# Up product of a hybrid block's FFN: six weight operands made during row 7 of the output product, two T2 sums and one evacuation brought forward on VectorE

## The chip, the cores and the metric

One core of one Trainium2 chip runs the whole program. The metric is the device time in microseconds (us), the median of several runs; lower is better. The engines are TensorE (PE in the profile), VectorE (DVE), ScalarE (ACT), GpSimd (POOL) and the DMA queue of SyncE (SP).

## The reference

One layer of a hybrid block: a token mixer (attention and a recurrent branch, merged and multiplied by `w_o`), then a convolutional feed-forward network (FFN). All arrays are fp32; there are 1024 tokens and 1024 channels, and `D_FF` is 2816.

```python
h = h + gate1[:, None, :] * mix                  # mix = merged @ w_o
u2 = modulate(rms_norm(h, ln2_g[l]), shift2, scale2)
h = h + gate2[:, None, :] * conv_ffn(u2, w_up[l], conv_w[l], conv_b[l], w_down[l])

def conv_ffn(u, w_up, conv_w, conv_b, w_down):
    a, b = jnp.split(u @ w_up, 2, axis=-1)
    a = conv(a, conv_w) + conv_b                 # depthwise, three tokens
    return (jax.nn.silu(a) * b) @ w_down
```

The change lies where the product with `w_o` (the output product) ends and the product with `w_up` (the Up product) begins.

## The kernel before

**fp32 in three passes.** An fp32 operand is split into a part `hi` (rounded to the fast matmul type, a cast on ScalarE) and a rest `lo` (operand minus `hi`, on VectorE; this document calls that instruction the operand's *lower*). Each product of two operands is made of hi·hi, lo·hi and hi·lo (`PARTS`).

**Output product.** `wo_do(t, k)` computes 128 tokens (row t, 0 to 7): 48 matmuls, 8 parts of the contraction in the outer loop (`kt`), two halves of the channels, three passes. The weights' lo parts lie in the slots `a0` to `a7`, slot `a<kt>` being read in part kt. `wo_row(t, ps)` follows: on VectorE times `g1b` (L1459) and plus h (L1460), on ScalarE the sum of squares (L1461), then a store by SP. `norm2` adds the two halves' sums of squares (L1400) and makes 1/rms on ScalarE (L322, L323); `scale_row` multiplies the row by it (L1408; for row 7 one half on VectorE, L1411, and one on ScalarE, L1412).

**Activations of the Up product.** `turn2` transposes the scaled rows on TensorE into PSUM banks (`tr`), four 128 by 128 blocks per channel block, and evacuates them with the modulation's scale and shift: on ScalarE (L1429), or on VectorE by `evac_dve` (L1436) for the places in `by_dve`. The first half of the tokens gives B11 and B21, made earlier; the second half gives B12 (`U[0]`) and B22 (`U[1]`), four channel blocks of 512 tokens each.

**Up product in seven products.** It is done in 22 slices i; in each the 2 by 2 blocks A (weights) and B (activations) are multiplied in seven products instead of eight, with sums formed beforehand:

```python
OPS = {1: ("A11", "B11"), 2: ("A12", "B21"), 3: ("S4", "B22"), 4: ("A22", "T4"), 5: ("S1", "T1"), 6: ("S2", "T2"),
       7: ("S3", "T3")}
```

S1 = A21 + A22, S2 = S1 - A11, S3 = A11 - A21, S4 = A12 - S2; T3 = B22 - B12 (`diff`), T2 = T3 + B11, T4 = B21 - T2, T1 = B22 - T2. The T operands are made once, while slices 0 and 1 run, and serve all slices; the A and S operands are made for each slice. A product (`up_product`) is 12 matmuls of 128x128 by 128x512 on a bank X, Y or W. `plan` lists the products (i, k):

```python
plan = [(i, k) for ks in ((1, 2), (7,), (6,)) for i in range(2) for k in ks]
plan += [(0, 4), (0, 5), (1, 5), (1, 4), (0, 3), (1, 3)] + [(2, k) for k in (1, 7, 6, 2, 4, 5)]
```

So products 1 and 2 of slices 0 and 1 come first, with the transposes between them, then product 7 of both (T3), product 6 of both (T2), (0, 4) with T4, (0, 5) and (1, 5) with T1, and so on.

**Operands.** `up_ahead(n)` makes the A and S operands of the first n products of the plan: `up_make` forms a sum if one is needed (S2 at L1515, S4 at L1518), casts `hi` on ScalarE (L1522) and returns the lower (L1526) as a function that the caller runs later. From the fifth operand on they are put in the slots `a0` to `a5` in turn, which until then hold lo weights of the output product. `up_evac` takes results out of PSUM (L1600 and L1605 to L1609), `up_first` and `later` schedule the convolution of a slice: `conv_last` (L1563, ScalarE), `conv_taps` (L1560, VectorE), `silu`, `gated`; the number n in `up_first` says after how many products the chain begins. The load of slice i + 2 is issued by the lower of S4 of slice i, into buffers of slice i that are free again.

**Order.** From before row 5 on, VectorE, ScalarE and SP run exactly in the order of the code (a manual schedule), as TensorE does throughout; an instruction that waits holds all that stand behind it on its engine.

Of the kernel before, what the change touches and what calls it, by code (L numbers as in the profile page):

```python
# [12 lines left out]
ALU = mybir.AluOpType  # L13
# [121 lines left out]
def hybrid_block(ctx: ExitStack, tc: tile.TileContext, a, out):  # L135
# [13 lines left out]
    def f32(ap):  # L149
        return ap.bitcast(F32)  # L150

    tt, stt, ts = nc.vector.tensor_tensor, nc.vector.scalar_tensor_tensor, nc.vector.tensor_scalar
# [167 lines left out]
    def rms_rstd(dst, ssq):  # L320

        nc.scalar.activation(dst, ssq, AF.Ln, scale=1.0 / D, bias=epsr[:, 0:1])  # L322
        nc.scalar.activation(dst, dst, AF.Exp, scale=-0.5)  # L323
# [50 lines left out]
    with ExitStack() as es:  # L374
# [66 lines left out]
        with tc.tile_pool(name="st", bufs=1) as st, tc.tile_pool(name="stp", bufs=2, space=PS) as stp, \  # L441
                tc.manual_schedule(engines={mybir.EngineType.SP, mybir.EngineType.DVE, mybir.EngineType.Activation}):
            ssq = st.tile([128, 8], F32, name="ssq")
# [597 lines left out]
    with tc.manual_schedule(engines={mybir.EngineType.DVE, mybir.EngineType.Activation}):  # L1041
# [7 lines left out]
        def slot(free):  # L1049
            while not free:  # L1050
                yield 100
            yield free.popleft() - weave.now
# [219 lines left out]
    if "rest" in marks:  # L1272
        g, m = (gsp.tile([128, NH], F32, tag="sp0", name=f"rest{k}") for k in range(2))
        i = nc.scalar.activation(g, marks["rest"], AF.Abs)
# [13 lines left out]
    ssq = hp.tile([128, 32], F32, name="ssq2")  # L1288

    def pairs(tags, name, dt=F32R):  # L1290

        ts_ = [slot(tag, f"{name}_{tag}", dt) for tag in tags]
        return [ts_[k // 2][:, k % 2 * NH : k % 2 * NH + NH] for k in range(2 * len(tags))]

    def halves(tags, name):

        n = len(tags) // 2
        return [pairs(tags[x * n : x * n + n], f"{name}{x}") for x in range(2)]
# [98 lines left out]
    def norm2(t0, t1):  # L1397

        hs, rs = slice(t0, t1), slice(8 + t0, 8 + t1)
        tt(ssq[:, rs], ssq[:, rs], ssq[:, hs], op=ALU.add)  # L1400
        rms_rstd(ssq[:, rs], ssq[:, rs])
# [3 lines left out]
    def scale_row(t, dst=None):  # L1405
        r = ssq[:, 8 + t : 9 + t]
        if dst is None:
            ts(h_sb[t], h_sb[t], r, None, op0=ALU.mult)  # L1408
            dst = [h_sb[t][:, c * NH : c * NH + NH] for c in range(2)]
        else:  # L1410
            ts(dst[0], h_sb[t][:, 0:NH], r, None, op0=ALU.mult)  # L1411
            nc.scalar.activation(dst[1], h_sb[t][:, NH:], AF.Copy, scale=r)  # L1412
        normed[t] = dst
# [20 lines left out]
    def evac_dve(n):  # L1434
        dst, ps, A, B = put[n]
        ts(dst, ps, A, B, op0=ALU.mult, op1=ALU.add)  # L1436
# [17 lines left out]
    def wo_row(t, ps):  # L1454

        for c in range(2):
            cs = slice(c * NH, c * NH + NH)
            x, h = row_tmp[2 * t + c] if t < 5 else hp.tile([128, NH], F32, tag=("dg", "xq")[c], name=f"wo{t}_{c}", bufs=(1, 5)[c]), h_sb[t][:, cs]
            tt(x, ps[c], g1b[:, cs], op=ALU.mult)  # L1459
            tt(h, h, x, op=ALU.add)  # L1460
            nc.scalar.activation(x, h, AF.Square, accum_out=ssq[:, 8 * c + t : 8 * c + t + 1])  # L1461
        nc.sync.dma_start(d_h[t], h_sb[t])
# [3 lines left out]
    def T_tiles(key, tags):  # L1466
        T[key] = halves(tags, key)
# [23 lines left out]
    def up_sums(i):  # L1491

        r = up_raw[i]
        r["S3"] = hp.tile([128, NH], F32, tag="s", name=f"s{i}", bufs=2)
        tt(r["S3"], r["A11"], r["A21"], op=ALU.subtract)
        tt(r["A21"], r["A21"], r["A22"], op=ALU.add)
# [9 lines left out]
    def up_make(i, key):  # L1506

        r = up_raw[i]
        if key == "S3":
            if "S3" not in r:  # L1510
                up_sums(i)
            src = r["S3"]
        elif key == "S2":
            src = r["A11"]
            tt(src, r["A21"], src, op=ALU.subtract)  # L1515
        elif key == "S4":
            src = r["A12"]
            tt(src, src, r["A11"], op=ALU.subtract)  # L1518
        else:
            src = r["A21" if key == "S1" else key]  # L1520
        hi, lo = up_place(f"{key}_{i}")
        nc.scalar.copy(hi, src)  # L1522
        up_ops[i, key] = hi, lo

        def lower():
            tt(lo, src, f32(hi), op=ALU.subtract)  # L1526
            if key == "S4" and i + 2 < NFF:
                up_load(i + 2)

        return lower  # L1530
# [17 lines left out]
    def later(n, f, *args):  # L1548

        due.append((done["run"] + n, f, args))  # L1550
# [27 lines left out]
    def up_first(i):  # L1578

        o = ups[i]  # L1580
        ab = o["ab"] = slot(f"m{6 + i % 2}", f"ab{i}", n=S + 2)
        o["c"] = slot(("e0", "a6", "m14", "m15")[i % 4], f"c{i}")
        nc.vector.memset(ab[:, 0:2], 0.0)
        tt(ab[:, 2 : 2 + NH], o["W"], o["x1"], op=ALU.add)
        n = {0: 2, 1: 5}.get(i, 0)
        later(n, conv_last, i, 0, ab[:, 2 : 2 + NH])
        later(n + 1, conv_taps, i, 0)
        later(n + 2, silu, i, 0)
        later(n + 3, gated, i, 0)

    def up_evac(i, k):
        o = ups[i]
        if k in (1, 7, 6):
            key = {1: "x1", 7: "Z", 6: "U"}[k]
            tag, bufs = ("dg", 1) if (i, k) == (1, 6) else ("xq", 5)
            if k == 7 and i < 2:
                o[key] = early[i]
            else:
                o[key] = hp.tile([128, NH], F32, tag=tag, name=f"{key}_{i}", bufs=bufs)
            nc.scalar.copy(o[key], o["Y" if k == 7 else "X"])  # L1600
        elif k == 2:
            if i > 1:
                up_first(i)
        elif k == 4:
            o["C21"] = tt(o["U"], o["Y"], o["U"], op=ALU.add)  # L1605
        elif k == 5:
            o["C22"] = tt(o["Z"], o["X"], o["Z"], op=ALU.add)
        else:
            nc.scalar.copy(o["ab"][:, 2 + NH :], o["X"])  # L1609
            conv_last(i, 1, o["X"])  # L1610
            n = {0: 3, 1: 6}.get(i, 0)
            later(n, conv_taps, i, 1)
            later(n + 1, silu, i, 1)
            later(n + 2, gated, i, 1)
# [39 lines left out]
    def up_ahead(n):  # L1654
        lower = []
        while done["made"] < min(len(plan), n):
            i, k = plan[done["made"]]
            lower.append(up_make(i, OPS[k][0]))
            done["made"] += 1
        return lower  # L1660
# [50 lines left out]
    def wo_do(t, k):  # L1711
        ps = [bank(k + c, f"wo{t}_{c}") for c in range(2)]
        for kt in range(KT):
            wo_mm(t, kt, ps)
        return ps
# [16 lines left out]
    def turn_first(kts, ks):  # L1732
        turn2(0, kts, ks, [uf[kt] for kt in kts], split_evac=True)
        for kt in kts:
            split(*(T["B11" if kt < 4 else "B21"][x][kt % 4] for x in range(2)), uf[kt])
# [5 lines left out]
    for t, k in ((5, 2), (6, 6), (7, 4)):  # L1741
        ps = wo_do(t, k)
        if t < 7:

            up_sums(t - 5)
            for f in up_ahead(2 * (t - 4)):
                f()
        wo_row(t, ps)
        if t == 5:
            turn_first(range(4, 8), (4, 5, 0, 1))  # L1750
        elif t == 6:
            norm2(4, 7)
            for r in (4, 5, 6):
                scale_row(r)
# [3 lines left out]
    steps = up_to(len(plan))  # L1758
    t1, b21 = uf[0:4], uf[4:]
    U = [pairs(tags, f"u2{j}", F32) for j, tags in enumerate((("m8", "m9"), ("m10", "m11")))]  # L1760
    norm2(7, 8)
    scale_row(7, U[1][2:])
    T_tiles("T3", [f"h{k}" for k in range(4)])

    def T_split(key, srcs, sums=()):
# [10 lines left out]
    diff = pairs(("m2", "m3"), "diff", F32)  # L1776
    for n in range(4):
        up_evac(*next(steps))
        if n == 1:
            for f in up_ahead(8):  # L1780
                f()
        if n in (1, 2):
            kts = (0, 1) if n == 1 else (2, 3)
            turn2(1, [kt + 4 * j for kt in kts for j in range(2)], (2, 3, 4, 5), [U[j][kt] for kt in kts for j in range(2)],
                  rows=((0, 1, 2), (3,)) if n == 1 else ((0, 1, 2, 3),), by_dve=(1, 3) if n == 2 else ())
            for kt in kts:
                if n == 2:
                    evac_dve(2 * (kt % 2) + 1)
                tt(diff[kt], U[1][kt], U[0][kt], op=ALU.subtract)
                nc.scalar.copy(T["T3"][0][kt], diff[kt])  # L1790
            for kt in kts:
                tt(T["T3"][1][kt], diff[kt], f32(T["T3"][0][kt]), op=ALU.subtract)
    for kt in range(4):
        tt(U[0][kt], diff[kt], t1[kt], op=ALU.add)
    T_tiles("T2", [f"m{k}" for k in range(4)])
    T_split("T2", U[0])
# [13 lines left out]
    for i in range(4):  # L1810
        up_evac(*next(steps))
        if i > 1:
            up_first(i - 2)
# [274 lines left out]
```

## Time and profile before

| | |
|---|---|
| runs | 1642.08, 1642.18, 1642.57 us; median 1642.18 |
| profiled execution | 1642.93 us; its span, first to last instruction, 1641.1 us |
| TensorE busy | 1600.1 us, 98% of the span |
| VectorE, ScalarE, GpSimd busy | 1211.9, 827.7, 158.5 us |
| mean granted TensorE clock | 0.997 |
| last row of the output product ends, Up product starts | 997.0 us |
| product 6 of slice 2 starts | 1048.3 us |

In the rows of a timeline stand: start in us from the span's start, length in us, engine, line, operation, tile written <- tiles read, shapes, count of merged instructions and, in brackets, the engine's idle time before them with what ended it. SPq is the SP queue issuing a DMA. In a row of the windows view stand: the stretch, its length, busy time and instruction count of TensorE, its weight loads, VectorE, ScalarE and GpSimd, then granted clock, DMA share and GB/s. Tile names lose their numbers: `u_m` are the `U` tiles, `T_h` holds T3 or T4, `T_m` T2 or T1, `uf_e` B11, B21 and what is made in their place, `ur` raw weights, `tr` a transposed block in PSUM.

### The profile page before, as it was taken

To read this page: it belongs to the slowest core of one execution; us is meant where nothing else is said; L and a number is where in the kernel's file an instruction comes from. 1 tells how busy PE (TensorE), PEld (TensorE's weight loads), DVE (VectorE), ACT (ScalarE), POOL (GpSimd) and SP (SyncE) were. 2 spreads that over 40 slices of the span, in tenths; PEclk is the share of its full clock that TensorE was granted. 3 is DMA by queue.
4 is the path that set the end of the run, shared out by engine and by line. 5 is a ranking of instruction groups with operands and counts; after the bars stand their busy time and mean duration, and the time that the engine had idled before them with its cause. 6 is when DMAs were issued, how large, how long until landed. Compare 5 with 4: busy or idle time off the path is not lost.

```text
span 1641.1 us, 25961 instructions
## 1 busy us (share of the span) xinstructions
PE 1600.1 (98%) x9678; PEld 1332.6 (81%) x9678; DVE 1211.9 (74%) x2342; ACT 827.7 (50%) x1558; POOL 158.5 (10%) x189
## 2 busy tenths in 40 slices
PE   7999999999999999999999999999999999999998
PEld 7778778888978788888878888788888888888886
DVE  5786787878876536878678557887777777886677
ACT  5563344544455656777623335644444444555455
POOL 0011111112101011333122000000000000000000
PEclk9999999999999999999999999999999999999999
DMA  9487645543332346443197510232332332675363
GB/s 340 129 326 206 175 132 142 139 117 98 114 104 87 97 134 151 131 120 107 55 349 266 187 67 26 84 135 96 105 113 97 98 108 96 232 249 161 122 211 109
DMA packets 123542, 238.79 MB, mean 146 GB/s; under 512 B 42188, under 2 KB 51284, under 8 KB 123416
## 3 DMA queue, kind: packets, MB, share of 16 engines
q1 hardware_dynamic: 114936, 218.77, 41.0%
q0 software_dynamic: 8480, 18.37, 4.1%
q8 instruction: 76, 1.25, 0.3%
q14 instruction: 50, 0.41, 0.1%
HBM read 172.57 MB, written 64.50 MB: 144 GB/s over the span
## 4 chain that ended last, share of the span: by engine, by line
PE 59%; DVE 5%; ACT 3%; issue 1%; DMA 1%; SPq 0%; ACTq 0%; DVEq 0%
PE X L143 13%; PE D L143 13%; PE Y L143 6%; PE wo L143 5%; PE br L143 4%; PE gt L143 4%; PE rk_ps L143 4%; PE W L143 3%; PE ov L143 2%; PE lg L143 2%; PE tp L147 1%; DVE quads L1082 1%; DVE P L1092 1%; DVE tl L1122 0%; ACT P L1086 0%
## 5 line engine op out<-in xcount | busy, mean ns | idle before, releaser
L143 PE MATMUL D<-op,op 128*128 128x512 f32 x924 | 209.8, 389 | 0.0
L143 PEld LDWEIGHTS D<-op,op 128*128 128x128 f32 x924 | 173.3, 188 | 36.3 <-DVE op L1302 0.3
L143 PE MATMUL X<-T_m,S 128*128 128x512 f32 x440 | 107.8, 390 | 1.6 <-ACT T_m L1772 1.1
L143 PEld LDWEIGHTS X<-T_m,S 128*128 128x128 f32 x440 | 82.4, 188 | 20.4 <-ACT T_m L1772 2.5
L1301 ACT CAST op<-g 128x512 fp32r<-128x512 f32 x77 | 47.8, 621 | 74.1 <-PE D L143 50.3
L1302 DVE TENSOR_TENSOR op<-g,op 128x512 fp32r<-128x512 f32 x77 | 53.0, 688 | 41.3 <-ACT op L1301 41.3
L1560 DVE SCALAR_TENSOR_TENSOR c<-ab,vec,c 128x512 f32<-128x512 f32 x88 | 65.8, 749 | 18.4 <-ACT c L1563 16.8
L814 DVE TENSOR_TENSOR t<-E,M 128x60 f32<-128x60 f32 (+24 forms) x248 | 56.2, 226 | 27.7 <-DMA M<-sm 21.7
L1526 DVE TENSOR_TENSOR A<-ur,A 128x512 fp32r<-128x512 f32 x64 | 43.9, 687 | 38.8 <-ACT A L1522 38.6
L1526 DVE TENSOR_TENSOR S<-ur,S 128x512 fp32r<-128x512 f32 x66 | 45.5, 691 | 35.2 <-ACT S L1522 35.1
L1522 ACT CAST S<-ur 128x512 fp32r<-128x512 f32 x66 | 41.0, 622 | 55.8 <-DVE ur L1515 30.7
L298 DVE TENSOR_TENSOR lo_in<-raw_in,hi_in 128x512 fp32r<-128x512 f32 x84 | 57.5, 724 | 15.6 <-PE gt L143 4.8
L143 PE MATMUL Y<-T_h,A 128*128 128x512 f32 x264 | 63.7, 390 | 0.3 <-ACT T_h L1772 0.3
L143 PE MATMUL Y<-T_h,S 128*128 128x512 f32 x264 | 63.6, 390 | 0.4 <-ACT T_h L1790 0.4
L1522 ACT CAST A<-ur 128x512 fp32r<-128x512 f32 x64 | 39.7, 622 | 43.2 <-PE X L143 31.3
L1122 DVE TENSOR_TENSOR tl<-tp,th 128x512 fp32r<-128x512 f32 (+1 forms) x80 | 49.9, 630 | 15.3 <-ACT th L1119 15.1
L296 ACT CAST hi_in<-raw_in 128x1024 fp32r<-128x1024 f32 x42 | 43.8, 1047 | 34.1 <-PE qk L143 13.9
L143 PE MATMUL W<-B_f,A 128*128 128x512 f32 x252 | 60.6, 389 | 0.0
L143 PE MATMUL X<-B_b,A 128*128 128x512 f32 x252 | 60.5, 389 | 0.0
L816 DVE TENSOR_TENSOR E<-E,t 128x60 f32<-128x60 f32 (+24 forms) x248 | 55.7, 225 | 6.3
L143 PEld LDWEIGHTS Y<-T_h,S 128*128 128x128 f32 x264 | 49.5, 188 | 11.1 <-ACT T_h L1790 0.8
L143 PEld LDWEIGHTS Y<-T_h,A 128*128 128x128 f32 x264 | 49.5, 188 | 11.0 <-ACT T_h L1772 0.7
(488 smaller groups left out, 4137.2 us busy)
## 6 DMA issues: line engine op xcount, KB each, us to landing
raw_in<-in_w_in SPq DMA_DIRECT2D x50, 512.0 KB
wm<-in_w_mod SPq DMA_DIRECT2D x48, 512.0 KB
ur<-in_w_up SPq DMA_DIRECT2D x44, 512.0 KB
g<-d_g SPq DMA_DIRECT2D x35, 512.0 KB
d_g<-gs SPq DMA_DIRECT2D x44, 256.0 KB
d_g<-c SPq DMA_DIRECT2D x33, 256.0 KB
d_st<-qh SPq DMA_DIRECT2D x64, 128.0 KB
stA<-d_st POOLq DMA_DIRECT2D x8, 1024.0 KB, 7.9
```

What stands on the lines that cost most here:

```text
L143: nc.tensor.matmul(o, lhsT, rhs, start=start, stop=stop, skip_group_check=more)
L147: nc.tensor.transpose(o, i, eye)
L296: nc.scalar.copy(hi, raw)
L298: nc.vector.tensor_tensor(lo[:, c : c + NH], raw[:, c : c + NH], f32(hi[:, c : c + NH]), op=ALU.subtract)
L814: tt(tv, E32[:, 0:J, s : s + 1].to_broadcast([128, J, W]), M32[:, s : s + 1, s + 1 : 32].to_broadcast([128, J, W]), op=ALU.mult)
L816: tt(E32[:, 0:J, s + 1 : 32], E32[:, 0:J, s + 1 : 32], tv, op=ALU.add)
L1122: tt(tl[:, 0:w], tp[:, 0:w], f32(th[:, 0:w]), op=ALU.subtract)
L1301: nc.scalar.copy(hi, src)
L1302: tt(lo, src, f32(hi), op=ALU.subtract)
L1522: nc.scalar.copy(hi, src)
L1526: tt(lo, src, f32(hi), op=ALU.subtract)
L1560: stt(c, ab[:, x + hf * NH : x + hf * NH + NH], V("conv_w", 22 * x + i), c, op0=ALU.mult, op1=ALU.add)
```

## The change

1. For row 7, between its product and `wo_row`, `up_ahead(10)` makes the next six operands: S3 and S2 of slices 0 and 1, A22 and S1 of slice 0. Their casts and S2 sums are issued there with the two S3 lowers; the S2 lowers follow the sum of row 7's statistics (L1765, formerly L1400), the other two lowers follow row 7's scaling.
2. In the first group of transposed blocks `by_dve=(1,)` moves the evacuation of block 4 from ScalarE to VectorE, ahead of the first difference; the T2 sum of block 0 is formed right behind its difference, that of block 1 behind the T3 lowers.
3. In `up_first`, n of slice 0 becomes 3: its convolution chain starts one product later.

```diff
-        n = {0: 2, 1: 5}.get(i, 0)
+        n = {0: 3, 1: 5}.get(i, 0)
...
             up_sums(t - 5)
             for f in up_ahead(2 * (t - 4)):
                 f()
+        else:
+            lows = up_ahead(10)
+            for f in lows[:2]:
+                f()
         wo_row(t, ps)
...
-    norm2(7, 8)
+    tt(ssq[:, 15:16], ssq[:, 15:16], ssq[:, 7:8], op=ALU.add)
+    for f in lows[2:4]:
+        f()
+    rms_rstd(ssq[:, 15:16], ssq[:, 15:16])
     scale_row(7, U[1][2:])
+    for f in lows[4:]:
+        f()
...
     for n in range(4):
         up_evac(*next(steps))
-        if n == 1:
-            for f in up_ahead(8):
-                f()
         if n in (1, 2):
             kts = (0, 1) if n == 1 else (2, 3)
             turn2(1, [kt + 4 * j for kt in kts for j in range(2)], (2, 3, 4, 5), [U[j][kt] for kt in kts for j in range(2)],
-                  rows=((0, 1, 2), (3,)) if n == 1 else ((0, 1, 2, 3),), by_dve=(1, 3) if n == 2 else ())
+                  rows=((0, 1, 2), (3,)) if n == 1 else ((0, 1, 2, 3),), by_dve=(1, 3) if n == 2 else (1,))
             for kt in kts:
-                if n == 2:
+                if n == 2 or kt == 0:
                     evac_dve(2 * (kt % 2) + 1)
                 tt(diff[kt], U[1][kt], U[0][kt], op=ALU.subtract)
+                if kt == 0:
+                    tt(U[0][0], diff[0], t1[0], op=ALU.add)
                 nc.scalar.copy(T["T3"][0][kt], diff[kt])
             for kt in kts:
                 tt(T["T3"][1][kt], diff[kt], f32(T["T3"][0][kt]), op=ALU.subtract)
-    for kt in range(4):
+            if n == 1:
+                tt(U[0][1], diff[1], t1[1], op=ALU.add)
+    for kt in (2, 3):
         tt(U[0][kt], diff[kt], t1[kt], op=ALU.add)
```

In the order of ScalarE, from the statistics of rows 4 to 6 (L323) to row 7's scaled half (L1412) and on, before (`S_0` and `S_1` are sums of slices 0 and 1, `s` and `ur` the raw weights, `wo` row 7, `x_0` the evacuated product 1):

```order
L323 ACTIVATE ssq_9265<-ssq_9265 128x3
L1461 ACTIVATE wo_0_10648,ssq_9265<-h_sb_10302 128x512
L1461 ACTIVATE wo_1_10652,ssq_9265<-h_sb_10302 128x512
L322 ACTIVATE ssq_9265<-ssq_9265,epsr 128x1
L323 ACTIVATE ssq_9265<-ssq_9265 128x1
L1412 ACTIVATE u_m_10661<-h_sb_10302,ssq_9265 128x512
L1600 COPY x_0_10686<-X_10673 128x512
L1522 CAST S_0_10688<-s_10472 128x512
L1522 CAST S_1_10704<-s_10572 128x512
L1522 CAST S_0_10707<-ur_10304 128x512
L1522 CAST S_1_10710<-ur_10416 128x512
```

and now:

```order
L323 ACTIVATE ssq_9265<-ssq_9265 128x3
L1522 CAST S_0_10648<-s_10472 128x512
L1522 CAST S_1_10650<-s_10572 128x512
L1522 CAST S_0_10653<-ur_10304 128x512
L1522 CAST S_1_10656<-ur_10416 128x512
L1522 CAST A_0_10658<-ur_10305 128x512
L1522 CAST S_0_10660<-ur_10305 128x512
L1461 ACTIVATE wo_0_10664,ssq_9265<-h_sb_10302 128x512
L1461 ACTIVATE wo_1_10668,ssq_9265<-h_sb_10302 128x512
L322 ACTIVATE ssq_9265<-ssq_9265,epsr 128x1
L323 ACTIVATE ssq_9265<-ssq_9265 128x1
L1412 ACTIVATE u_m_10677<-h_sb_10302,ssq_9265 128x512
```

Four casts that stood behind row 7's scaling, and two that stood further down, now stand ahead of row 7's squares; each of them waits for TensorE as well, since it writes a slot that held weights of the output product.

On VectorE, from the sum of row 7's statistics (`ssq`) to the T3 lowers, before (`diff` is T3, `u_m` holds the transposed blocks):

```order
L1400 TENSOR_TENSOR ssq_9265<-ssq_9265 128x1
L1411 TENSOR_SCALAR u_m_10661<-h_sb_10302,ssq_9265 128x512
L1526 TENSOR_TENSOR S_0_10688<-s_10472,S_0_10688 128x512
L1515 TENSOR_TENSOR ur_10304<-ur_10305,ur_10304 128x512
L1515 TENSOR_TENSOR ur_10416<-ur_10417,ur_10416 128x512
L1526 TENSOR_TENSOR S_1_10704<-s_10572,S_1_10704 128x512
L1526 TENSOR_TENSOR S_0_10707<-ur_10304,S_0_10707 128x512
L1526 TENSOR_TENSOR S_1_10710<-ur_10416,S_1_10710 128x512
L1789 TENSOR_TENSOR diff_m_10671<-u_m_10660,u_m_10658 128x512 x2
L1792 TENSOR_TENSOR T_h_10669<-diff_m_10671,T_h_10667 128x512 x2
```

and now:

```order
L1765 TENSOR_TENSOR ssq_9265<-ssq_9265 128x1
L1526 TENSOR_TENSOR S_0_10653<-ur_10304,S_0_10653 128x512
L1526 TENSOR_TENSOR S_1_10656<-ur_10416,S_1_10656 128x512
L1411 TENSOR_SCALAR u_m_10677<-h_sb_10302,ssq_9265 128x512
L1526 TENSOR_TENSOR A_0_10658<-ur_10305,A_0_10658 128x512
L1526 TENSOR_TENSOR S_0_10660<-ur_10305,S_0_10660 128x512
L1436 TENSOR_SCALAR u_m_10676<-tr_4_10722,A_96,m_95 128x512
L1795 TENSOR_TENSOR diff_m_10691<-u_m_10676,u_m_10674 128x512
L1797 TENSOR_TENSOR u_m_10674<-diff_m_10691,uf_e_10380 128x512
L1795 TENSOR_TENSOR diff_m_10691<-u_m_10676,u_m_10674 128x512
L1800 TENSOR_TENSOR T_h_10689<-diff_m_10691,T_h_10687 128x512 x2
L1802 TENSOR_TENSOR u_m_10674<-diff_m_10691,uf_e_10380 128x512
```

The two S2 sums (L1515) and the S3 lowers have gone ahead of row 7; the evacuation of block 4 and two T2 sums have come in around the differences. Two lowers (`A_0`, `S_0` of `ur_10305`) that stood behind the T2 lowers and behind the T4 lowers now stand here.

On ScalarE, before the copy of product 1 of slice 2 (`x_2`, after which bank X may be written again), before:

```order
L1522 CAST S_2_11031<-ur_10961 128x512
L1609 COPY ab_11026<-X_10745 128x512
L1563 ACTIVATE c_11027<-X_10745,vec 128x512
L1522 CAST A_2_11048<-ur_10961 128x512
L1563 ACTIVATE c_11003<-ab_11002,vec 128x512
L1600 COPY x_2_11065<-X_11052 128x512
```

and now:

```order
L1522 CAST S_2_11031<-ur_10961 128x512
L1609 COPY ab_11026<-X_10753 128x512
L1563 ACTIVATE c_11027<-X_10753,vec 128x512
L1522 CAST A_2_11048<-ur_10961 128x512
L1600 COPY x_2_11064<-X_11051 128x512
L1522 CAST A_2_11066<-ur_10962 128x512
L1563 ACTIVATE c_11003<-ab_11002,vec 128x512
```

The first convolution step of slice 0 (`c` from `ab`) has moved behind the copy and one more cast.

## The prediction

> **What bounds the kernel now.** I read the page first, then the waits of TensorE, then the timelines of TensorE, VectorE (DVE) and ScalarE (ACT) around the start of the Up product.
>
> ```profile
> span 1641.1 us, 25961 instructions
> PE 1600.1 (98%) x9678; PEld 1332.6 (81%) x9678; DVE 1211.9 (74%) x2342; ACT 827.7 (50%) x1558; POOL 158.5 (10%) x189
> 1050.00:1633.00 583.00, 583.00 (x2572) 482.49 (x2572) 450.21 (x712) 284.25 (x501) 0.00 (x0) 1.00 0.41 136
> ```
>
> TensorE is the bound: busy for 98% of the span, and in the windows view for all 583 us from 1050 to 1633. Whatever TensorE gains before 1050 therefore reaches the end unless a new wait arises. Its timeline where the Up product starts (start, length, count, idle before and who ended it):
>
> ```profile
> 996.98 2.89 PE L143 MATMUL X<-B_b,A 128*128 128x512 f32 x12
> 1003.81 0.60 PE L147 MATMUL tr<-cst,u_m 128*128 128x128 f32 x4
> ...
> 1011.47 1.75 PE L143 MATMUL Y<-T_h,S 128*128 128x512 f32 x7
> 1013.62 4.17 PE L143 MATMUL Y<-T_h,S 128*128 128x512 f32 x17 [0.40 <-ACT T_h L1790]
> 1017.62 5.60 PE L143 MATMUL X<-T_m,S 128*128 128x512 f32 x24
> 1023.06 0.84 PE L143 MATMUL Y<-T_h,A 128*128 128x512 f32 x3
> 1024.20 2.34 PE L143 MATMUL Y<-T_h,A 128*128 128x512 f32 x9 [0.30 <-ACT T_h L1772]
> 1027.44 1.02 PE L143 MATMUL X<-T_m,S 128*128 128x512 f32 x2 [0.90 <-ACT T_m L1772]
> ...
> 1031.34 1.98 PE L143 MATMUL X<-T_m,S 128*128 128x512 f32 x8
> ...
> 1048.34 1.89 PE L143 MATMUL X<-T_m,S 128*128 128x512 f32 x7 [0.52 <-ACT x L1600]
> ```
>
> The 24 matmuls from 1017.62 to 1023.06 start 0.2267 us apart; that is the dense pace. From 1011.47 to the sixth product of slice 2 at 1048.34 there are twelve products, 144 matmuls: dense, 32.64 us, so 1044.11. **TensorE loses 48.34 - 44.11 = 4.23 us here**: 0.56 before 1013.62 (7 x 0.2267 would end at 1013.06), 0.15 restarting behind it (17 end at 1017.47, the next starts at 1017.62), 0.46 before 1024.20, 1.20 before 1027.44, 1.18 inside the T1 product (12 from 1027.44 would end at 1030.16, the next product starts at 1031.34), 0.68 before 1048.34. Each wait is for ScalarE, but ScalarE itself waits for VectorE, which is the true queue:
>
> ```profile
> 1011.31 0.80 DVE L1436 TENSOR_SCALAR u_m<-tr,A,m 128x512 f32<-128x512 f32 x1
> 1012.22 0.69 DVE L1789 TENSOR_TENSOR diff_m<-u_m,u_m 128x512 f32<-128x512 f32 x1
> 1014.21 2.49 DVE L1794 TENSOR_TENSOR u_m<-diff_m,uf_e 128x512 f32<-128x512 f32 x4
> 1019.02 0.68 DVE L1526 TENSOR_TENSOR A<-ur,A 128x512 fp32r<-128x512 f32 x1
> 1024.79 0.68 DVE L1526 TENSOR_TENSOR S<-ur,S 128x512 fp32r<-128x512 f32 x1
> 1025.39 2.49 DVE L1804 TENSOR_TENSOR uf_e<-u_m,u_m 128x512 f32<-128x512 f32 x4
> 1012.95 0.62 ACT L1790 CAST T_h<-diff_m 128x512 fp32r<-128x512 f32 x1 [0.89 <-DVE diff_m L1789]
> 1026.77 2.35 ACT L1772 CAST T_m<-uf_e 128x512 fp32r<-128x512 f32 x4 [1.13 <-DVE uf_e L1804]
> ```
>
> Four independent Vector instructions take 2.49, so they start 0.60 apart. The last T3 difference (1012.22) sets the cast at 1012.95 and so the wait before 1013.62 (cast end 1013.57 plus 0.05); from there VectorE has no idle time until L1804 at 1025.39, which sets the T1 casts.
>
> **The change, part by part.** Room in front:
>
> ```profile
> 991.73 2.08 DVE L1408 TENSOR_SCALAR h_sb<-h_sb,ssq 128x1024 f32<-128x1024 f32 x3 [0.60 <-ACT ssq L323]
> 996.50 0.69 DVE L1459 TENSOR_TENSOR wo<-wo,g1b 128x512 f32<-128x512 f32 x1 [2.69 <-PE wo L143]
> 997.23 0.69 DVE L1460 TENSOR_TENSOR h_sb<-h_sb,wo 128x512 f32<-128x512 f32 x1
> 997.84 0.68 DVE L1459 TENSOR_TENSOR wo<-wo,g1b 128x512 f32<-128x512 f32 x1
> 1000.03 0.16 DVE L1400 TENSOR_TENSOR ssq<-ssq 128x1 f32<-128x1 f32 x1 [0.79 <-ACT wo L1461]
> 1000.79 0.48 DVE L1411 TENSOR_SCALAR u_m<-h_sb,ssq 128x512 f32<-128x512 f32 x1 [0.60 <-ACT ssq L323]
> 997.95 0.64 ACT L1461 ACTIVATE wo<-h_sb 128x512 f32<-128x512 f32 x1 [6.25 <-DVE h_sb L1460]
> 1001.42 0.57 ACT L1600 COPY x<-X 128x512 f32<-128x512 f32 x1
> 1003.87 1.22 ACT L1522 CAST S<-ur 128x512 fp32r<-128x512 f32 x2 [0.84 <-DVE ur L1515]
> 1004.99 2.78 ACT L1429 ACTIVATE u_m<-tr,m,A 128x512 f32<-128x512 f32 x4
> ...
> 1025.50 33.41 SPq L1488 DMA_DIRECT2D ur<-in_w_up  x6
> ```
>
> *Six casts before row 7's squares.* ScalarE idles 6.25 us before 997.95. The T1 row puts casts (2.35 - 0.62)/3 = 0.58 apart; the third waits for the first S2 sum, done at 994.5 (below), so the last ends at 994.5 + 3 x 0.58 + 0.62 = 996.9 at the latest. They write a0 to a5, which hold row 7's lo weights, so each waits for TensorE: row 7 starts 48 x 0.2267 = 10.88 before 996.98, at 986.10, and is through with one such tile every 1.36 us: a0 at 987.7, a5 at 994.5. Cost 0, cover 1.0.
>
> *Two S2 sums and two S3 lowers before row 7's scaling.* VectorE idles 2.69 before 996.50. From 993.81 (991.73 + 2.08) the four end at 993.81 + 3 x 0.60 + 0.69 = 996.30. Cost 0, cover 0.20; beyond it row 7 is late one for one. *Two S2 lowers behind L1765* take 1.2, of which 0.60 lies in the idle time before L1411: that starts at about 1001.4 and ends at 1001.9. TensorE wants row 7 at 1003.81, cover 1.9. *A22 and S1 lowers* run from 1001.9 to 1003.2, before the first transpose is out. SP's first load of slice 2 waited for the S1 lower at 1025.50; it goes out at about 1003.3, with nothing queued behind it that waits: cost 0.
>
> *T3.* The four transposes from 1003.81 start 0.11 apart: tr_0 is out at 1004.08, tr_4 at 1004.19. ScalarE is free at 1001.99 instead of 1004.99, and evacuates tr_0, tr_1, tr_5 0.67 apart (L1429: (2.78 - 0.78)/3), done at 1006.2. VectorE: tr_4 at 1004.23; first difference 0.91 later (1011.31 to 1012.22), 1005.14; its T2 sum, which needs that result, 0.73 later (as 996.50 to 997.23), 1005.87; second difference 1006.48; T3 lo 1007.09; second lo behind its cast, 1007.85; second T2 sum 1008.46; tr_6 1009.06; difference 1009.97; tr_7 1010.58; **last difference 1011.49 instead of 1012.22**. Its cast ends 1.35 later, at 1012.84; TensorE wants it at 1013.06: the 0.56 and the 0.15 go, cover 0.2.
>
> *T2, T4, T1.* From the last difference to L1804 there were 13.17 us (1012.22 to 1025.39). Two T2 sums and the lowers at 1019.02 and 1024.79 are gone, 4 x 0.60: 10.77, so L1804 starts at 1022.26, 3.13 earlier. The 0.46 wait at T4 goes with it (its cast comes some 2.5 us earlier, its product 0.71: 1011.47 + 48 x 0.2267 = 1022.35). The T1 product can start dense at 1011.47 + 60 x 0.2267 = 1025.07 and wants its fourth cast at 1025.75; that ended 3.73 behind L1804 (1026.77 + 2.35 - 1025.39), so 1022.26 + 3.78 = 1026.04: **0.29 stays, 0.15 for the restart**, against 1.20 + 1.18.
>
> *The copy before 1048.34.* It hangs on the same VectorE chain, 48.34 - 25.39 = 22.95 behind L1804. Between the two the instructions of VectorE and ScalarE keep their order, but for one that the change of n takes out of the copy's way:
>
> ```profile
> 1046.99 0.82 ACT L1563 ACTIVATE c<-ab,vec 128x512 f32<-128x512 f32 x1
> 1047.70 0.58 ACT L1600 COPY x<-X 128x512 f32<-128x512 f32 x1
> ```
>
> That saves 0.71: ready at 1022.26 + 22.24 = 1044.50; TensorE arrives at 1044.11 + 0.44 = 1044.55. The wait is gone, cover 0.05.
>
> *Sum.* 48.34 - 44.55 = 3.79 us. The profiled execution took 1642.93 (span 1641.1), so 1639.1; it lies 0.75 above the median of the runs, 1642.18, which gives **1638.4**. Bounds: all 4.23 at best (1637.9). Each 0.1 by which the VectorE chain is slower costs 0.1. The new kind of instruction, an evacuation on VectorE between others, lies between ScalarE's 0.67 and VectorE's 0.91; I take 0.91, measured next to the place. With 0.67 three evacuations would save 0.7, more than the stall left.
>
> [...]
>
> **The rivals.** 0.2% of 1642.18 is 3.28 us, about what a measurement of this kernel can tell from no change.
>
> *A: the casts wait for all of row 7.* The order shows only a wait on TensorE. If it were for the whole product, which ends at about 997.1 (the next starts at 996.98), the S3 lowers, which stand ahead of row 7's L1459, would start at 997.85 and L1459 at 999.07, 2.57 late; L1411 ends at 1004.4, the lowers at 1005.6, the first difference is at 1006.5, 1.37 behind forecast: gain 48.34 - 45.87 = 2.47, **1639.7**. Against: by the code each tile is last read an eighth at a time.
>
> *B: the wait returns at the copy.* Its cover is 0.05. If ScalarE's queue keeps it where it was relative to L1804, it is ready at 1045.21: gain 3.13, **1639.05**. For: five in-order instructions stand between the S2 cast of slice 2 and the copy. Against: the cut instruction stood directly before it.
>
> *C: slower.* If those casts wait until the next two products are through as well (996.98 + 24 x 0.2267, 1002.6 with the last one's tail), L1459 starts at 1004.5, 8.0 late, TensorE waits 6 us for row 7, and the first difference comes at 1011.9, 6.8 late: 1044.50 + 6.8 = 1051.3, 2.96 later than now, **1645.1**. It decides from casts that start after 999.7. Against: a0 to a5 have no reader in those products.
>
> **How the numbers follow.** Forecast 0.76, A 0.10, B 0.10, C 0.04. Faster by over 0.2% is the forecast, 0.76; A and B lie within 0.2%, 0.20; slower 0.04. The range goes from all 4.23 gone, less 0.1 for the spread of the runs (1637.8), to just beyond A (1639.8); it leaves out C.
>
> **What would show it.** In the changed profile: no idle before the Y product at 1011.5 nor before T4; L1459 of row 7 still at 996.5; ScalarE's first tr evacuation at 1004.1; last T3 difference near 1011.5; T1 differences near 1022.3; the sixth product of slice 2 at 1044.4 to 1044.7; TensorE without waits after 1050. I am wrong if L1459 moves past 997, if TensorE waits for row 7's transposes, or if the T1 product waits over 0.8 us.

## The result and the profile after

The changed kernel took 1640.44 us (median of 13 runs, 1637.25 to 1643.03), the kernel before 1643.38 on the same chip (13 runs, 1642.08 to 1646.14). The ratio is 0.998, 95% interval 0.9972 to 0.9987. So it is faster, by 3.3 us as the ratio has it (2.1 to 4.6), and the time forecast, 1638.4, is 2.0 below what was measured and outside its range. The profiled execution took 1639.56.

The page's first lines, and the row of the windows view for the long stretch behind the change:

```profile
span 1637.8 us, 25963 instructions
PE 1600.6 (98%) x9678; PEld 1334.4 (81%) x9678; DVE 1214.5 (74%) x2343; ACT 827.8 (51%) x1557; POOL 157.4 (10%) x189
1050.00:1630.00 580.00, 580.00 (x2560) 479.91 (x2558) 448.27 (x709) 282.68 (x500) 0.00 (x0) 1.00 0.41 136
```

TensorE is about as busy as before (1600.6 us against 1600.1) in a span 3.3 shorter: only idle time went. It still has no gap behind 1050, so nothing gained ahead of that is given back.

TensorE's timeline around the start of the Up product:

```profile
997.44 2.89 PE L143 MATMUL X<-B_b,A 128*128 128x512 f32 x12
...
1011.98 5.63 PE L143 MATMUL Y<-T_h,S 128*128 128x512 f32 x24
1017.44 5.60 PE L143 MATMUL X<-T_m,S 128*128 128x512 f32 x24
1022.88 2.88 PE L143 MATMUL Y<-T_h,A 128*128 128x512 f32 x12
1025.60 2.33 PE L143 MATMUL X<-T_m,S 128*128 128x512 f32 x8
...
1031.42 2.88 PE L143 MATMUL Y<-T_h,A 128*128 128x512 f32 x12
...
1042.30 2.88 PE L143 MATMUL Y<-T_h,S 128*128 128x512 f32 x12
1045.02 2.98 PE L143 MATMUL X<-T_m,S 128*128 128x512 f32 x12
```

The waits for T3 and T4, the one in front of T1 and the one before product 6 of slice 2 have gone: their rows, broken in two before, are whole. Only inside the T1 product something is left: its 24 matmuls start at 1025.60 and the next product at 1031.42, 5.82 instead of 24 x 0.2267 = 5.44, so 0.38. From the first matmul of the Up product to product 6 of slice 2 it was 51.36 us (996.98 to 1048.34) and is 47.58 (997.44 to 1045.02). **The stage gained 3.78 us; 3.79 was forecast.**

VectorE and ScalarE there:

```profile
994.21 1.29 DVE L1515 TENSOR_TENSOR ur<-ur,ur 128x512 f32<-128x512 f32 x2
995.41 1.29 DVE L1526 TENSOR_TENSOR S<-s,S 128x512 fp32r<-128x512 f32 x2
996.96 0.69 DVE L1459 TENSOR_TENSOR wo<-wo,g1b 128x512 f32<-128x512 f32 x1 [0.27 <-PE wo L143]
1004.69 0.81 DVE L1436 TENSOR_SCALAR u_m<-tr,A,m 128x512 f32<-128x512 f32 x1 [1.23 <-PE tr L147]
1005.61 0.69 DVE L1795 TENSOR_TENSOR diff_m<-u_m,u_m 128x512 f32<-128x512 f32 x1
1006.34 0.69 DVE L1797 TENSOR_TENSOR u_m<-diff_m,uf_e 128x512 f32<-128x512 f32 x1
1006.95 0.69 DVE L1795 TENSOR_TENSOR diff_m<-u_m,u_m 128x512 f32<-128x512 f32 x1
1011.96 0.69 DVE L1795 TENSOR_TENSOR diff_m<-u_m,u_m 128x512 f32<-128x512 f32 x1
1022.74 2.49 DVE L1814 TENSOR_TENSOR uf_e<-u_m,u_m 128x512 f32<-128x512 f32 x4
992.08 1.13 ACT L1522 CAST S<-s 128x512 fp32r<-128x512 f32 x2
994.97 1.24 ACT L1522 CAST S<-ur 128x512 fp32r<-128x512 f32 x2 [1.76 <-PE wo L143]
996.63 0.61 ACT L1522 CAST S<-ur 128x512 fp32r<-128x512 f32 x1
1004.58 2.12 ACT L1429 ACTIVATE u_m<-tr,m,A 128x512 f32<-128x512 f32 x3 [2.13 <-PE tr L147]
1044.34 0.60 ACT L1600 COPY x<-X 128x512 f32<-128x512 f32 x1
1003.53 46.62 SPq L1488 DMA_DIRECT2D ur<-in_w_up  x5
```

Row 7's L1459 stands 0.48 ahead of the first matmul of the Up product, as it did before (996.50 to 996.98), and VectorE's idle time ahead of it has shrunk from 2.69 to 0.27: the four moved instructions filled it and no more. The rows lie 0.46 later than forecast, because in this execution row 7 itself ended 0.46 later.

### The profile page after: what moved, and what is told of

The parts are those of the page before. It is cut to its first block, busy times and chain, and to the rows that moved or that the text cites. A ratio compares the mean times of both kernels' runs of the same rounds, so it can differ in the third digit from the quotient of the medians.

```text
span 1637.8 us, 25963 instructions
## 1 busy us (share of the span) xinstructions
PE 1600.6 (98%) x9678; PEld 1334.4 (81%) x9678; DVE 1214.5 (74%) x2343; ACT 827.8 (51%) x1557; POOL 157.4 (10%) x189
## 4 chain that ended last, share of the span: by engine, by line
PE 71%; DVE 6%; ACT 2%; issue 1%; DMA 1%; SPq 1%; POOL 0%; DVEq 0%; POOLq 0%; ACTq 0%
PE X L143 15%; PE D L143 13%; PE Y L143 7%; PE gt L143 6%; PE wo L143 5%; PE br L143 4%; PE rk_ps L143 4%; PE W L143 4%; PE ps_rkv L143 3%; PE ov L143 2%; PE lg L143 2%; PE tp L147 1%; PE v L143 1%; PE sp L143 1%; DVE quads L1082 1%
```

## The experiments

Theory 1, as the expectations call it, has two halves. The stage is set by one chain of VectorE and ScalarE work, and the change shortens it by what the prediction says; and the time of an execution is otherwise set ahead of the Up product, in the first 500 us, which the change doesn't touch and which differ from execution to execution by more than the gain. The rivals are named in each expectation.

All measurements of the stage in one table. "Start" is the first matmul of the Up product; "to T3" runs from there to the first T3 product; the losses are start-to-start times over 0.2267 per matmul; "in front of T1" includes T4. Each row can be read from TensorE's timeline of that kernel. The loss of 2.79 holds 1.61 that isn't a wait, as told below.

| kernel | start | to T3 | T3 | in front of T1 | in T1 | copy | stage |
|---|---|---|---|---|---|---|---|
| before | 996.98 | 14.49 | 0.71 | 1.66 | 1.18 | 0.68 | 51.36 |
| before, again | 998.02 | 14.53 | 0.67 | 1.68 | 1.18 | 0.68 | 51.37 |
| changed | 997.44 | 14.53 | 0.03 | 0 | 0.38 | 0 | 47.58 |
| changed, again | 998.09 | 14.53 | 0 | 0 | 0.39 | 0 | 47.57 |
| six operands alone | 1000.13 | 14.53 | 0 | 0.27 | 1.17 | 0.69 | 49.30 |
| T order alone | 996.27 | 14.65 | 2.09 | 0.47 | 1.18 | 0.68 | 51.70 |
| changed, n = 2 | 998.03 | 14.53 | 0.02 | 0 | 0.36 | 0.68 | 48.23 |
| n = 3 alone | 999.60 | 14.53 | 0.66 | 1.67 | 2.79 | 0 | 52.30 |
| operands behind row 7 | 998.53 | 15.03 | 0.42 | 0 | 0.41 | 0 | 48.50 |

**The changed kernel again**, no edit.

> The changed kernel once more, unaltered. Measure of the stage: from the first matmul of the Up product to the first one of product 6 of slice 2 (before 1048.34 - 996.98 = 51.36 us, changed 1045.02 - 997.44 = 47.58). Theory 1 (the gain is that stage's 3.78, all of it reaches the end, and what differs beside it is how long the program's first 500 us take, which differ from execution to execution in code that the change does not touch): stage 47.5 to 47.7 again, TensorE without a wait after 1050, but the place where row 7 ends anywhere from 995 to 1000; ratio to the kernel before 0.9965 to 0.9988. Rival (the change itself costs about 0.5 us ahead of row 7 or gives it back after 1050): row 7 ends 0.4 to 0.6 us later than in every profile of the kernel before, or the stretch from product 6 of slice 2 to the end is 0.4 us longer than before.

It took 1640.23 (7 runs, 1637.78 to 1642.69), the kernel before 1643.81 (29 runs, 1641.57 to 1647.06), ratio 0.9978 (0.9966 to 0.999). The stage is the same to 0.01, and the start of the Up product lies 0.65 later than in the first profile. Neither sign of the rival is there: from product 6 of slice 2 to the last matmul it takes 584.89, and the starts of the changed kernel (997.44, 998.09 and, in a third profile, 996.05) lie to both sides of those of the kernel before (996.98 and 998.02).

**The six operands alone**: the T order and n as before. The diff is against the changed kernel.

```diff
-        n = {0: 3, 1: 5}.get(i, 0)
+        n = {0: 2, 1: 5}.get(i, 0)
...
-                  ... by_dve=(1, 3) if n == 2 else (1,))
+                  ... by_dve=(1, 3) if n == 2 else ())
...
-                if kt == 0:
-                    tt(U[0][0], diff[0], t1[0], op=ALU.add)
...
-            if n == 1:
-                tt(U[0][1], diff[1], t1[1], op=ALU.add)
-    for kt in (2, 3):
+    for kt in range(4):
```

> The six operands during row 7 alone (no evacuation of block 4 on VectorE, T2 sums where they were, n = 2). Theory 1 (one VectorE chain sets the stage; every instruction taken out of it counts once): ScalarE's four evacuations start at about 1004.1 + 0.5 instead of 1004.99, the last difference about 1 us earlier; two lowers are gone from the chain behind it, two T2 sums stay, the copy keeps its 0.71: stage 48.8 to 49.3, that is 2.1 to 2.6 of the 3.78. Rival (the parts are independent, the operands only fill idle time and the T order brings most): stage 50.2 or more.

1641.83 (1639.94 to 1644.87), ratio 0.999 (0.9981 to 0.9999). The stage took 49.30, a gain of 2.06, and the rival, which wanted 50.2 or more, falls. In its timelines of VectorE and TensorE:

```profile
1008.75 0.69 DVE L1795 TENSOR_TENSOR diff_m<-u_m,u_m 128x512 f32<-128x512 f32 x1 [2.60 <-ACT u_m L1429]
1010.09 0.69 DVE L1795 TENSOR_TENSOR diff_m<-u_m,u_m 128x512 f32<-128x512 f32 x1 [0.65 <-ACT u_m L1429]
1029.73 1.94 PE L143 MATMUL X<-T_m,S 128*128 128x512 f32 x6 [0.18 <-ACT T_m L1781]
1049.42 3.03 PE L143 MATMUL X<-T_m,S 128*128 128x512 f32 x12 [0.53 <-ACT x L1600]
```

With the operands out of the way VectorE stands idle for 2.60 and 0.65 until ScalarE has evacuated the transposed blocks; the T1 product and the copy lose as much as before (1.17 and 0.69). This is the room that the second part of the change fills.

**The order of T alone**: evacuation and T2 sums moved, operands and n as before. The diff is against the changed kernel.

```diff
-        else:
-            lows = up_ahead(10)
-            for f in lows[:2]:
-                f()
...
-    for f in lows[4:]:
-        f()
...
+        if n == 1:
+            for f in up_ahead(8):
+                f()
```

> The evacuation of block 4 and the two T2 sums alone (operands as before, n = 2). Theory 1: ScalarE and VectorE are still held until 1005 to 1006 by the S2 and S3 operands, so the chain cannot start earlier; one evacuation and two sums more stand ahead of the last difference, so the wait for T3 grows from 0.56 to about 2 us, and what the two sums save later pays it back: stage 51.1 to 51.6, no gain (0.0 +- 0.3). Rival (parts independent): two sums of 0.60 less in the chain, stage 50.2.

1642.94 (1642.34 to 1646.02), ratio 0.9996 (0.9987 to 1.0005): no difference. The stage is 0.34 longer than before, a little worse than expected.

```profile
1005.45 0.80 DVE L1436 TENSOR_SCALAR u_m<-tr,A,m 128x512 f32<-128x512 f32 x1
1014.45 4.16 PE L143 MATMUL Y<-T_h,S 128*128 128x512 f32 x17 [1.36 <-ACT T_h L1792]
```

The moved evacuation now has to stand behind the six lowers and sums of the operands: it starts 9.18 after the Up product's start (1005.45 - 996.27) and 7.25 in the changed kernel (1004.69 - 997.44). T3 comes later by what was put ahead of it, a loss of 2.09 instead of 0.71, and the gain in front of T1 (1.66 to 0.47) doesn't make up for it.

**The changed kernel with n = 2.**

```diff
-        n = {0: 3, 1: 5}.get(i, 0)
+        n = {0: 2, 1: 5}.get(i, 0)
```

> The changed kernel with n = 2 for slice 0 as before. Theory 1: the copy of product 1 of slice 2 ended at 1044.94 with TensorE arriving at 1045.0, so with the convolution step (0.71) in front of it again the copy is 0.65 late: stage 48.2 to 48.4, 0.6 to 0.8 lost. Rival (the cover was larger than thought, or ScalarE makes the step up): stage 47.6.

1640.89 (1639.57 to 1644.16), ratio 0.9982 (0.9973 to 0.9991). The wait at the copy is back, and nothing else:

```profile
1046.27 3.02 PE L143 MATMUL X<-T_m,S 128*128 128x512 f32 x12 [0.52 <-ACT x L1600]
```

The four kernels that follow ran on one chip beside the kernel before (1643.29, 27 runs, 1640.95 to 1645.57).

**The kernel before, profiled again**, no edit.

> The kernel before, profiled once more. Theory 1 (the level of an execution is set before the Up product; the stage itself is fixed by one chain of VectorE and ScalarE work): from the first matmul of the Up product to the first matmul of product 6 of slice 2 it takes 51.3 to 51.4 us, as in the first profile (51.36), and the rest up to the last matmul 584.9 us, while the first matmul of the Up product lies anywhere from 996 to 1000 us, not at 996.98 again; its time differs from the other profile's by the difference of those starts, within 0.1 us. Rival (the spread arises all along the program, each stage taking a little more or less): start, stage and rest each differ by some tenths.

1643.7 (8 runs, 1642.16 to 1644.85), ratio 1.0002 (0.9992 to 1.0012). The profiled execution took 1643.97 against 1642.93 in the first profile, 1.04 more; its Up product starts 1.04 later:

```profile
998.02 2.89 PE L143 MATMUL X<-B_b,A 128*128 128x512 f32 x12
1049.39 3.04 PE L143 MATMUL X<-T_m,S 128*128 128x512 f32 x12 [0.52 <-ACT x L1600]
```

The stage is 51.37. What makes these two executions of one kernel differ lies ahead of the Up product, all of it.

**The operands behind row 7's steps** instead of ahead of them, in the changed kernel. They are the six of the change: S3 and S2 of slices 0 and 1, A22 and S1 of slice 0.

```diff
-        else:
+        wo_row(t, ps)
+        if t == 7:
             lows = up_ahead(10)
             for f in lows[:2]:
                 f()
-        wo_row(t, ps)
```

> The changed kernel with the casts and low parts of slices 2 and 3 of operands 0 to 2 issued behind the steps of the last row of the output product instead of ahead of them. Theory 1 (one chain of VectorE and ScalarE work sets the waits in front of T3, T1 and the copy; work put ahead of row 7 lies beside row 7's matmuls, which need VectorE only at their end): the six VectorE instructions now start after row 7's last step and the chain runs 1.0 to 1.5 us later; waits come back in front of T3 (about 0.4 us) and T1 (about 0.5) and before product 6 of slice 2; the stage takes 48.4 to 49.2 us instead of 47.58, and the time is 0.8 to 1.6 us above the changed kernel's. Rival A turned round (what is ahead of row 7 delays row 7 itself, so that moving it behind brings row 7 forward): the Up product starts earlier by some tenths and the stage stays within 0.2 of 47.58.

1640.9 (10 runs, 1638.83 to 1643.47), ratio 0.9987 (0.9978 to 0.9996). Rows of VectorE and TensorE:

```profile
998.05 0.69 DVE L1459 TENSOR_TENSOR wo<-wo,g1b 128x512 f32<-128x512 f32 x1 [2.69 <-PE wo L143]
1000.71 1.28 DVE L1515 TENSOR_TENSOR ur<-ur,ur 128x512 f32<-128x512 f32 x2
1005.13 0.49 DVE L1411 TENSOR_SCALAR u_m<-h_sb,ssq 128x512 f32<-128x512 f32 x1 [0.47 <-ACT ssq L323]
1005.67 0.78 PE L147 MATMUL tr<-cst,u_m 128*128 128x128 f32 x4 [0.16 <-DVE u_m L1411]
998.53 2.89 PE L143 MATMUL X<-B_b,A 128*128 128x512 f32 x12
```

Row 7's L1459 stands 0.48 ahead of the Up product here too (998.05 to 998.53): the work ahead of row 7 never delayed it. What changes is that row 7's scaling waits for the sums and casts, TensorE for row 7 (0.50 in "to T3") and T3 (0.42). The stage is 48.50, 0.92 longer; T1 lost 0.03 and not the 0.5 expected, and no wait came back before product 6 of slice 2, where one was expected.

**n = 3 alone**, in the kernel before (the diff of the n = 2 kernel turned round): the convolution chain of slice 0 begins one product later, and nothing else changes.

> The kernel before with one number changed: three steps of the low parts of the second half instead of two in the first group of slice 0 (n = 3), nothing else. Theory 1: it takes away only the wait of the copy before product 6 of slice 2 (0.68 us and the 0.11 behind it): stage 50.6 to 50.7 us instead of 51.36, the three other waits (T3, T4, T1) as before. Rival (the three parts of the change are worth the same alone as together, 3.78 less 2.06 for the operands less -0.34 for the order of T): this part would have to be worth about 2.0 us, stage 49.3.

1642.86 (10 runs, 1640.48 to 1646.37), ratio 0.9997 (0.9988 to 1.0006). The wait at the copy is gone, 0.68, as expected; yet the profiled stage is 52.30, not 50.65, because the T1 product lost 1.61 more. The windows view and TensorE's timeline say why:

```profile
1026.00:1032.00 6.00, 4.57 (x16) 2.47 (x15) 5.91 (x11) 4.65 (x9) 0.00 (x0) 1.00 0.28 87
1032.00:1036.00 4.00, 4.00 (x11) 3.11 (x11) 4.00 (x8) 2.86 (x6) 0.00 (x0) 0.57 0.00 0
1030.07 1.02 PE L143 MATMUL X<-T_m,S 128*128 128x512 f32 x2 [0.88 <-ACT T_m L1772]
1033.48 1.91 PE L143 MATMUL X<-T_e,S 128*128 128x512 f32 x4
```

As a mix of 1.00 and 0.50 the 0.57 means 4.00 x 0.43 / 0.50 = 3.4 us at half clock (in the first profile of the changed kernel the clock is 0.50 in every microsecond from 44 to 50 us), and four matmuls take 1.91 instead of the 1.07 of four others at 1037.39, behind that stretch. The same waits stood in both profiles of the kernel before, and there the clock stayed at full (second profile, the same stretch, 1.6 earlier because its Up product starts 1.6 earlier):

```profile
1024.40:1030.40 6.00, 4.57 (x16) 2.47 (x15) 5.91 (x11) 4.62 (x9) 0.00 (x0) 1.00 0.29 87
1030.40:1034.40 4.00, 4.00 (x18) 3.31 (x19) 4.00 (x8) 2.90 (x6) 0.00 (x0) 1.00 0.00 0
```

So 52.30 - 1.61 = 50.69 belongs to n, and the rival, which wanted 49.3, falls: the parts of the change are not worth the same alone as together. 2.06 - 0.34 + 0.68 is 2.40; together they bring 3.78.

**Sixteen more idle matmuls in the start phase** of the changed kernel, then, on another chip and beside the changed kernel itself, **21 more** and **sixteen again**. The idle matmuls (`warm`) compute nothing that is used.

```diff
-                warm((6, 40)[i])
+                warm((6, 56)[i])
```

> The changed kernel with sixteen more idle matmuls (56 instead of 40) in the start phase, in the 2 to 3 us at 39 to 42 us in which TensorE waits for VectorE's sum of the modulation; nothing else. Theory 1 (the level is set in the first 500 us; the half-clock spell of 6.8 us at 42 to 50 us, which stands in every profile so far, follows from that idle time): the spell is gone or half as long, the sixteen sums behind it take 0.18 us each instead of 0.35, the low product starts 1.0 to 1.5 us earlier than the 46.7 to 47.8 us of the other profiles, and the time is 0.5 to 1.5 us below the changed kernel's; stage still 47.6. Rival 1 (the spell comes whatever TensorE does there, or what follows is paced by VectorE): the low product starts at most 0.5 earlier and the time is the changed kernel's within its spread. Rival 2 (the added matmuls are in the way): the sums start later than 42.7 us, and the time is 0.5 to 1 us longer.

> The changed kernel with 61 idle matmuls in the start phase instead of 40 (56 left TensorE 0.93 us without work at 41.8 us and a half-clock spell of 3.4 us behind it instead of 6.8). Theory 1 (the spell answers to the idle time): with under 0.3 us of it left, no half-clock spell stands between 30 and 55 us; the low product starts at 46.0 to 46.5 us; the time is that of 56 idle matmuls or up to 0.5 us below. Rival (the spell at 44 us comes from the low load of the sixteen thin matmuls themselves, not from the gap ahead of them): a spell of 3.4 us stays, and nothing is gained over 56.

> The changed kernel with 56 idle matmuls once more, beside the changed kernel itself on the same chip. Theory 1: 0.5 to 2.5 us below the changed kernel's median (2.6 was between medians of different groups of runs; the profile shows 1.2 to 1.4 up to 190 us), spell of 3.4 us and low product at about 46.5 us again. Rival (the gain was the draw of five runs, since the profiled execution had lost it again by its later waits, at 264 us): the medians differ by less than 0.5.

> The changed kernel itself, as the companion of the two kernels with more idle matmuls. By both theories: 1639.5 to 1641 us median, 2.5 to 4.5 below the kernel before; stage 47.6, rest 584.9; a half-clock spell of 6.8 us at 42 to 44 us; first matmul of the Up product at 996 to 1000 us.

| kernel | median | runs | ratio to before |
|---|---|---|---|
| 56 idle | 1637.58 | 5, 1636.26 to 1639.73 | 0.9966 (0.9954 to 0.9979) |
| 56 idle, again | 1638.33 | 5, 1637.16 to 1638.92 | 0.9966 (0.9954 to 0.9978) |
| 61 idle | 1639.51 | 11, 1636.68 to 1642.16 | 0.9974 (0.9964 to 0.9984) |
| changed (40), beside the last two | 1639.86 | 11, 1638.15 to 1642.65 | 0.9976 (0.9968 to 0.9985) |

Windows of the start, first of the changed kernel (its first profile), then with 56, with 61, and of the changed kernel beside them:

```profile
38.00:44.00 6.00, 4.17 (x26) 3.88 (x24) 4.47 (x4) 2.10 (x2) 0.00 (x0) 0.94 0.34 135
44.00:52.00 8.00, 8.00 (x29) 7.11 (x30) 6.07 (x12) 3.00 (x5) 0.00 (x0) 0.62 0.00 1
```

```profile
38.00:44.00 6.00, 5.41 (x36) 5.12 (x35) 4.65 (x5) 2.10 (x2) 0.00 (x0) 1.00 0.32 126
44.00:52.00 8.00, 7.31 (x29) 5.91 (x29) 7.08 (x14) 3.50 (x6) 0.00 (x0) 0.79 0.00 1
```

```profile
38.00:44.00 6.00, 6.00 (x43) 5.98 (x42) 4.02 (x4) 2.10 (x2) 0.00 (x0) 1.00 0.25 97
44.00:52.00 8.00, 7.55 (x26) 5.58 (x26) 7.70 (x15) 3.67 (x7) 0.00 (x0) 0.79 0.02 4
```

```profile
38.00:44.00 6.00, 3.96 (x27) 3.68 (x25) 4.86 (x4) 2.10 (x2) 0.00 (x0) 1.00 0.37 145
44.00:52.00 8.00, 8.00 (x33) 5.85 (x32) 6.86 (x14) 3.12 (x6) 0.00 (x0) 0.79 0.00 1
```

The idle matmuls fill the gap (busy 4.17 to 5.41 and 6.00 of 6; 6.00 also with 56 again), and half clock in the two stretches falls from 6 x 0.06 / 0.5 + 8 x 0.38 / 0.5 = 6.8 us to 8 x 0.21 / 0.5 = 3.4. But it doesn't go away without the gap, so what was expected of 61 is refuted, and its rival, that the sixteen thin matmuls (128x1) bring the spell, fits; and the changed kernel alone shows 3.4 there as well in its last profile, with the gap, where 6.8 was expected. So the shorter spell can't be put down to the idle matmuls. The low product (tile `low`), the first useful one behind the thin matmuls, starts at 46.51, 46.64 (56) and 45.41 (61), against 47.75, 46.74 and 46.41 in the changed kernel: the gain is no larger than the spread, and less than the 1.0 to 1.5 expected of 56. The stage is 47.57 to 47.59 in all four. The kernel with 56 is faster than the kernel before in both groups of runs; beside the changed kernel, in the second, its median is 1.53 lower, and all five of its runs lie under all but one of the other's eleven. But why 56 and not 61 is not settled, and the intervals of the ratios overlap.

**Where executions differ.** The table gives the time at which TensorE starts its n-th matmul (the first is n = 0), less that in the first profile of before, worked out from the traces:

| n-th matmul (us in before) | 540 (122.3) | 1200 (230.1) | 1500 (264.1) | 3300 (430.1) | 3900 (497.4) | 6900 (1002.7) |
|---|---|---|---|---|---|---|
| before, again | -0.77 | 0.91 | -0.58 | 0.44 | 0.16 | 1.04 |
| changed | 0.21 | 0.50 | 0.63 | 0.73 | 0.24 | 0.47 |
| changed, again | -1.08 | 1.20 | -0.29 | 0.03 | 0.98 | 1.12 |
| six operands alone | -0.47 | -1.30 | -1.23 | -1.16 | 2.79 | 3.15 |
| n = 3 alone | -0.15 | 0.27 | 1.31 | 1.65 | 2.14 | 2.62 |

The first 6600 matmuls are the same code in all of them. Most of the differences arise ahead of 500 us, at a few places. The second half of theory 1 holds less strictly than its 500 us: of the 1.04 of the kernel before, 0.27 comes between 497 and 566 us and 0.63 between 566 and 640. From 640 us to the Up product no row of the table moves by more than 0.4. The largest step, 3.95 in the kernel with six operands alone, stands beside half clock, in its windows view:

```profile
460.00:465.00 5.00, 2.96 (x7) 2.17 (x8) 1.32 (x8) 2.89 (x6) 1.26 (x1) 0.69 0.53 157
465.00:472.00 7.00, 7.00 (x47) 5.22 (x46) 6.36 (x21) 5.26 (x9) 0.00 (x0) 0.50 0.29 85
```

That is 5 x 0.31 / 0.5 + 7 = 10.1 us at half clock, with 2.04 us of idle time where it begins. Half clock also stands beside the next largest steps up: "before, again" (1.68) and "changed, again" (2.28 from 122 to 230 us) step up between 176 and 190 us, and these two alone have a granted clock of 0.96 from 160 to 200 us, about 40 x 0.04 / 0.5 = 3.2 us at half clock, where the other rows and the first profile of before have 1.00. By 264 us both have lost 1.49 of it again. Another step has no such spell beside it (n = 3 alone, 1.04 between 230 and 264 us; the clock is 1.00 from 240 to 270): what it comes from stays open.

## Why the prediction was right, and where it was wrong

*Casts before row 7's squares: right.* None was held up by TensorE: the first two started at 992.08, right behind the statistics of rows 4 to 6, and the third at 994.97, just behind the first S2 sum (994.21 + 0.69 = 994.90), as forecast. Its row names TensorE for the wait, but the part of row 7 that reads its slot a2 was through at 997.44 - 10.88 + 3 x 1.36 = 990.64. The last ended at 996.63 + 0.61 = 997.24, forecast 996.9 + 0.46 at the latest. Rivals A and C fall: they needed row 7's L1459 2.57 and 8.0 later, and it moved by nothing against the Up product.

*The VectorE chain: right, row for row.* With the 0.46 added: first difference 1005.60 (measured 1005.61), last 1011.95 (1011.96), T1 differences 1022.72 (1022.74). The new evacuation took 0.92 to the next step (1004.69 to 1005.61); of the two prices the row's 0.91 held. With ScalarE's 0.67, by the prediction's estimate of 0.7 saved, the T1 wait would have gone; 0.38 of it stayed (forecast 0.44). The sum that depends on the difference starts 0.73 behind it (1005.61 to 1006.34), the next, independent step 0.61 behind the sum (1006.34 to 1006.95).

*The copy: right, with a cover as thin as forecast.* It ends at 1044.34 + 0.60 = 1044.94, and TensorE arrives at 1042.30 + 12 x 0.2267 = 1045.02. Rival B falls; without the change of n the wait is back at 0.68.

*Nothing late behind it: right.* From product 6 of slice 2 to the last matmul 584.91 us before and 584.88 after.

*The level: wrong, and this is the step that failed:* "it lies 0.75 above the median of the runs, 1642.18, which gives 1638.4", with "0.1 for the spread of the runs". Three runs that agreed within 0.5 were taken for the kernel's level and their agreement for its spread. The 91 runs of before in all the comparisons (the three among them) go from 1640.95 to 1648.38, median 1643.63, standard deviation 1.51; 70 of them lie above all three. The first profile was not 0.75 above its kernel's level but 0.70 below it. Without that step, 1642.93 - 3.79 = 1639.14, the forecast would have been 0.42 from the profiled execution, about the 0.46 by which its Up product starts later; that this start is so near is luck, since the starts of one kernel differ by over 1 us (996.98 and 998.02 before, 996.05 to 998.09 changed). From the wider level it would have been 1643.63 - 3.79 = 1639.84: of the 2.0 by which the forecast was too low, the level makes up 1643.63 - 1642.18 = 1.45. The 31 runs of the changed kernel have the median 1640.20. The difference of the two medians, 3.43, is uncertain by 0.7 to either side by resampling, and so takes in 3.78. The ratios of 0.998, 0.9978 and 0.9976 fit a gain of 0.23% within that spread.

## What to carry to other kernels

Read a stage from two points inside one trace: here it repeats to 0.02 us (51.36 and 51.37; 47.57 to 47.59), but for a spell of half clock (1.61 in n = 3 alone), while the whole time wanders by several (1640.95 to 1648.38 in the 91 runs of before). A time forecast needs the spread of executions, and three that agree don't show it; a profiled execution gives no more than one draw. And cost the parts of a reordering together: evacuation and sums moved up lose 0.34 alone, behind work that still stands in front of them, and gain 1.07 (49.30 to 48.23) once that work has gone elsewhere.

## What the runs showed of the hardware

The granted clock fell to half for about 3.4 us behind the waits at 1026 to 1032 us in the profile of n = 3 alone, for 6.8 behind 1.83 us of idle time at 42 us in the first profile of the changed kernel, and for 10.1 beside 2.04 us of idle time at 460 us in that of the six operands alone. It came in some executions and not in others with the same waits: the same 1.43 us of idle time in 6 were followed by half clock in the profile of n = 3 alone (0.57 in the next 4 us), which cost 1.61 us, and by none in the second profile of before (1.00). What starts a spell and sets its length isn't shown. Nor did a spell need much idle time: with 61 idle matmuls TensorE worked 13.55 of the 14 us from 38 to 52, sixteen of its matmuls thin ones, and 3.4 us of half clock came all the same. So these waits of TensorE cost their own length, and in one of the two profiles 1.61 us of half clock on top; that removing a wait removes the spell isn't shown.
